# RG-LRU gate products on four 64-by-64 tiles of the TensorE array, with the conv result also kept with its halves exchanged

## The chip, the cores and the metric

The kernel runs on one core of a Trainium2 chip. The metric is the device time of one execution in microseconds (us), the median of several. TensorE is written PE, VectorE DVE, ScalarE ACT, GpSimd POOL, SyncE SP, as in the profile; PEld is PE's weight loads, and a q behind a name is that engine's instruction queue (its DMA issues and waits).

## The reference, cut to what matters

One layer over 2048 latent tokens and 256 context tokens: a modulated norm, one projection into four groups, an S5 branch, an RG-LRU branch, gating, an output projection, a norm. The part that changes is the gates of the RG-LRU branch, 16 heads of 64 channels:

```python
xh = xc.reshape(bsz, length, LRU_HEADS, LRU_HEAD_DIM)
r = sigmoid(einsum("blhi,hij->blhj", xh, w_a) + b_a)
gi = sigmoid(einsum("blhi,hij->blhj", xh, w_x) + b_x)
log_a = -LRU_C * r * softplus(-lam)
a = exp(log_a)
bx = sqrt(-expm1(2.0 * log_a)) * (gi * xc)
h[t] = a[t] * h[t-1] + bx[t]        # both directions, from the context's final state
```

`xc` is the result of a depthwise convolution of width 4. Each direction has its own `w_a` and `w_x`, one 64x64 matrix per head.

## The kernel before, in words

The program writes its instructions from Python generators. A framework then orders them for each engine by priorities and its own estimate of readiness; the order is fixed when the program is built. Each engine works its list in that order.

The first 560 us are the first half of the input projection with its preparation. Then comes the stretch that the change touches. `projections(1, ...)` projects the second half of the tokens: 128 steps, each of 12 matmuls of 128x128x512, named `pp` (lines 249 to 251). Each new weight block is split on DVE into `whi` and `wlo` (lines 241 and 242). Beside it `lru` works through 8 blocks of 128 channels (two heads each). One block is:

- `load` fetches the projected block into `ut` (one buffer), on SP's queue, after small memsets on POOL;
- `conv` forms `xc` (one buffer): one ACT instruction (line 367), then three on DVE (line 370), each over all 2307 columns;
- `gates` multiplies `xc` by the gate matrices, for both directions `d` and for five column pieces (259 and four of 512). A 128x128 matrix `gw` holds two heads on its diagonal and zeros elsewhere. The products go to two PSUM pools of two buffers each (`pg`), and ACT takes the sigmoids to `rr` and `gi` (line 381);
- ACT makes a Tanh into `tt` (line 424), an Exp in `rr` (line 431) and a Sqrt in `tt` (line 439), with a table load wherever the function set changes;
- `finish`, which runs during the gates of the next block, makes the two scans on DVE (lines 387 to 394), their sum (line 397) and the product with the SiLU gate (line 401).

`rr`, `gi` and `tt` have three buffers each, so the second direction of a block waits until `finish` of the block before has released one.

At the end of the generators stands `build`. It takes 8 projection steps alone, then 100 steps with `lru` beside them at 1.5 of its yields a step, then 8 steps with `s5_inputs` of the first S5 half (matmuls `pw`), then the last 12 steps with the second half's `s5_inputs` and the first of two S5 scans. A scan has 144 dependent steps of three DVE instructions (lines 729 to 731); the two scans overlap in part. `s5_outputs` (matmuls `py`) of a half needs that half's whole scan. The RG-LRU part of the output projection (matmuls `po`, 12 a step) fills PE between them. Two more projections (`pgl`, `po`) end the program.

## Time and profile before

| | us |
|---|---|
| median of 3 runs | 1852.38 (1851.83 to 1858.7) |
| the profiled execution's own time | 1850.69 |
| its span, first to last instruction | 1848.9 |
| PE busy | 1731.9 (94%) |
| DVE busy | 1208.6 (65%) |
| ACT busy | 864.0 (47%) |
| gate matmuls (line 380), 320 records | 135.8 |

A 32-bit matmul stands in the trace as two records, each with its weight load, so the 160 gate products are 320 records. Busy times count the union of records, and PE's records overlap, so a busy PE is not PE at its peak; idle time of an engine that others do not wait for costs nothing. The mean granted TensorE clock is 0.975 of full speed.

### The profile page before, as it was taken

What the parts mean: (1) busy time and instruction counts of PE and PEld (TensorE: products, weight loads), DVE (VectorE), ACT (ScalarE), POOL (GpSimd) and SP (SyncE); (2) the same over time, 40 slices, a digit from 0 to 9 for tenths busy, and PEclk for the clock granted to TensorE, in tenths of its full rate; (3) what the DMA queues carried; (4) which work ended last, traced back from release to release, by engine and by line L of the source; (5) the groups of instructions that cost most, each with busy time, mean ns of one, the idle gap of its engine ahead of it and who ended that gap; (6) DMA issues with size and microseconds to landing.
All of it is one profiled execution on the core that took longest, in us unless ns stands there. A gap on an engine that the chain in (4) does not pass through costs nothing. (4 is left out here: it accounts for less than half of the span.)

```text
span 1848.9 us, 25310 instructions
## 1 busy us (share of the span) xinstructions
PE 1731.9 (94%) x9465; PEld 1410.6 (76%) x9465; DVE 1208.6 (65%) x1998; ACT 864.0 (47%) x1350; POOL 117.8 (6%) x236
## 2 busy tenths in 40 slices
PE   7889999999998999999989997959899999999998
PEld 2677888878886666666668886748788899998886
DVE  5789997861244799999982199999900166346663
ACT  3622222223653867776754986225455443222221
POOL 1011121110000000000000000000000000001111
PEclk9899999999999999999999998979899999999999
DMA  9566676655454234344467876328688767456553
GB/s 268 128 141 214 195 204 168 194 179 165 132 164 154 75 125 137 120 143 120 114 179 233 272 241 205 120 70 261 203 272 262 227 184 211 140 158 216 185 194 88
DMA packets 356974, 326.34 MB, mean 177 GB/s; under 512 B 123774, under 2 KB 300530, under 8 KB 351731
## 3 DMA queue, kind: packets, MB, share of 16 engines
q1 hardware_dynamic: 309680, 221.41, 42.3%
q0 software_dynamic: 15040, 60.31, 9.0%
q10 hardware_dynamic: 32130, 43.01, 6.7%
q8 instruction: 75, 1.23, 0.3%
q14 instruction: 49, 0.39, 0.1%
HBM read 211.47 MB, written 113.18 MB: 176 GB/s over the span
## 5 line engine op out<-in xcount | busy, mean ns | idle before, releaser
L249 PE MATMUL pp<-x,whi 128*128 128x512 f32 x1024 | 417.2, 408 | 2.5 <-ACT ust L299 1.7
L251 PE MATMUL pp<-x,wlo 128*128 128x512 f32 x1024 | 407.4, 398 | 5.3 <-DVE wlo L242 5.3
L250 PE MATMUL pp<-x,whi 128*128 128x512 f32 x1024 | 406.5, 397 | 0.0
L242 DVE TENSOR_TENSOR wlo<-wraw,whi 128x1024 fp32r<-128x1024 f32 x90 | 109.9, 1221 | 192.8 <-ACT whi L241 146.0
L249 PEld LDWEIGHTS pp<-x,whi 128*128 128x128 f32 x1024 | 193.4, 189 | 54.1 <-issue 10.8
L251 PEld LDWEIGHTS pp<-x,wlo 128*128 128x128 f32 x1024 | 193.2, 189 | 50.7 <-DVE wlo L242 5.7
L250 PEld LDWEIGHTS pp<-x,whi 128*128 128x128 f32 x1024 | 193.2, 189 | 46.0 <-issue 6.3
L380 PE MATMUL pg<-xc,gw 128*128 128x512 f32 (+1 forms) x320 | 135.8, 572 | 18.6 <-issue 12.4
L241 ACT CAST whi<-wraw 128x1024 fp32r<-128x1024 f32 x66 | 69.2, 1049 | 164.7 <-PE pp L250 127.1
L380 PEld LDWEIGHTS pg<-xc,gw 128*128 128x128 f32 x320 | 61.2, 197 | 79.1 <-issue 57.5
L729 DVE TENSOR_TENSOR p<-z,A 128x128 f32<-128x128 f32 x288 | 106.3, 381 | 6.1
L764 PE MATMUL py<-h,et 128*128 128x128 f32 x512 | 81.0, 282 | 28.8 <-ACT h L757 14.8
L249 PE MATMUL po<-x,whi 128*128 128x512 f32 x256 | 105.5, 412 | 2.3 <-ACT x L794 2.3
L251 PE MATMUL po<-x,wlo 128*128 128x512 f32 x256 | 102.1, 399 | 4.8 <-DVE wlo L242 4.8
L250 PE MATMUL po<-x,whi 128*128 128x512 f32 x256 | 101.8, 397 | 1.8 <-DVE x L795 1.8
L249 PE MATMUL po<-ws,yh 128*128 128x512 f32 x256 | 99.6, 389 | 0.0
L250 PE MATMUL po<-ws,yh 128*128 128x512 f32 x256 | 99.6, 389 | 0.0
L251 PE MATMUL po<-ws,yl 128*128 128x512 f32 x256 | 99.6, 389 | 0.0
L764 PEld LDWEIGHTS py<-h,et 128*128 128x128 f32 x512 | 69.4, 197 | 31.3 <-ACT h L757 16.6
L701 PE MATMUL pw<-u,wt 128*128 128x144 f32 x512 | 73.2, 302 | 16.2 <-DMA wt<-WD 10.7
L701 PEld LDWEIGHTS pw<-u,wt 128*128 128x128 f32 x512 | 70.4, 202 | 20.8 <-issue 12.1
L730 DVE TENSOR_TENSOR z<-z,p 128x64 f32<-128x64 f32 x288 | 75.1, 273 | 10.9 <-ACT z L705 4.8
(255 smaller groups left out, 3479.2 us busy)
## 6 DMA issues: line engine op xcount, KB each, us to landing
wraw<-in_w_in_dram SPq DMA_DIRECT2D x74, 512.0 KB
u<-ZU SPq DMA_DIRECT2D x64, 288.0 KB
ED<-E POOLq DMA_DIRECT2D x16, 1024.0 KB, 4.3
WD<-Wt POOLq DMA_DIRECT2D x32, 512.0 KB, 3.9
wt<-WD SPq DMA_DIRECT2D x32, 512.0 KB
et<-ED SPq DMA_DIRECT2D x32, 512.0 KB
mt<-KD SPq DMA_DIRECT2D x64, 192.0 KB
wmod<-in_w_mod_dram SPq DMA_DIRECT2D x8, 1024.0 KB
```

What stands on the lines that cost most here:

```text
L241: copy(out=hi, in_=raw)
L242: self.nc.vector.tensor_sub(out=lo, in0=raw, in1=hi)
L249: nc.tensor.matmul(ps, lhsT=whi(k), rhs=xhi(k), start=(k == 0), stop=False)
L250: nc.tensor.matmul(ps, lhsT=whi(k), rhs=xlo(k), start=False, stop=False)
L251: nc.tensor.matmul(ps, lhsT=wlo(k), rhs=xhi(k), start=False, stop=(k == KT - 1))
L380: nc.tensor.matmul(ps[:, :n], lhsT=gw[:, d, w, :], rhs=xc[:, o:o + n], start=True, stop=True)
L701: nc.tensor.matmul(pw[:, c, :], lhsT=w[:, gi, kt, c, :], rhs=u[:, kt, :], start=(kt == 0), stop=(kt == 1))
L729: v.tensor_mul(out=p, in0=cur.unsqueeze(1).to_broadcast([P, 2, 2, 32]), in1=self.A16[:, :, :, gs])
L730: v.tensor_add(out=nxt, in0=nxt, in1=p[:, 0])
L764: nc.tensor.matmul(o, lhsT=ms(e[:, i, gi]), rhs=h[:, i, :], start=False, stop=(i == 1))
```

## The change

The gate matrix loses its zero blocks: `gw` holds, on partitions 0 to 63, the two heads of `w_a` and, on 64 to 127, those of `w_x`. `conv` also keeps `xs`, a copy of `xc` with its two halves of 64 partitions exchanged, made by two DMAs on POOL's queue; it takes the buffer of `ut`. A piece of both gates is now four matmuls of 64x64, each on its own quarter of the array: rows by the gate, columns by the head. Rows 0 to 63 (the first gate) read head 0 from `xc` and head 1 from `xs`; rows 64 to 127 (the second) read head 0 from `xs` and head 1 from `xc`. The interleaving with the projection is renumbered from 100 steps at 1.5 to 108 at 1.4. The two memsets of `gw` go.

```diff
-            gw = le.tile([P, 2, 2, P], F32, tag="gw", bufs=2, name="gw")
-            nc.gpsimd.memset(gw[0:64, :, :, 64:128], 0.0)
-            nc.gpsimd.memset(gw[64:128, :, :, 0:64], 0.0)
+            gw = le.tile([P, 2, 2, 64], F32, tag="gw", bufs=2, name="gw")
...
-                    nc.sync.dma_start(out=gw[es, :, w, es], in_=src)
+                    nc.sync.dma_start(out=gw[w * 64:w * 64 + 64, :, e, :], in_=src)
...
-            return xc
+            xs = le.tile([P, N + 3], F32, tag="ut", bufs=1, name="xs")
+            for e in range(2):
+                nc.gpsimd.dma_start(out=xs[e * 64:e * 64 + 64, :N], in_=xc[64 - e * 64:128 - e * 64, :])
+            return xc, xs
...
             for o, n in [(0, X0)] + (tl_x if d == 0 else tl_x[::-1]):
+                pss = [pool.tile([P, 512], F32, tag=tag, name="pg") for pool, tag in ((self.psG, "g"), (self.psT, "t"))]
+                for w in range(2):
+                    ws = slice(w * 64, w * 64 + 64)
+                    for e in range(2):
+                        nc.tensor.matmul(pss[w][e * 64:e * 64 + 64, :n], lhsT=gw[ws, d, e, :],
+                                         rhs=xcs[(w + e) % 2][ws, o:o + n], start=True, stop=True,
+                                         tile_position=(64 * w, 64 * e))
                 for w, dst in ((0, rr), (1, gi)):
-                    pool, tag = ((self.psG, "g"), (self.psT, "t"))[w]
-                    ps = pool.tile([P, 512], F32, tag=tag, name="pg")
-                    nc.tensor.matmul(ps[:, :n], lhsT=gw[:, d, w, :], rhs=xc[:, o:o + n], start=True, stop=True)
-                    nc.scalar.activation(out=dst[:, o:o + n], in_=ps[:, :n], func=AF.Sigmoid, bias=bias[w])
+                    nc.scalar.activation(out=dst[:, o:o + n], in_=pss[w][:, :n], func=AF.Sigmoid, bias=bias[w])
...
-                    merge(islice(proj, 100), [lru, 1.5])
+                    merge(islice(proj, 108), [lru, 1.4])
```

**PE's order.** In the fifth block the gate products of before stand in one run of 13, from both gates in turn, and the projection's `pp` follow; these are the end of that run and what comes behind it.

```order
L380 MATMUL pg_5802<-xc_5708,gw_5652 128x512
L380 MATMUL pg_5805<-xc_5708,gw_5652 128x512
L380 MATMUL pg_5808<-xc_5708,gw_5652 128x512
L380 MATMUL pg_5811<-xc_5708,gw_5652 128x512
L380 MATMUL pg_5831<-xc_5708,gw_5652 128x259
L380 MATMUL pg_5834<-xc_5708,gw_5652 128x259
L380 MATMUL pg_5854<-xc_5708,gw_5652 128x512
L251 MATMUL pp_5872<-x2_4241,wlo_5796 128x512
L249 MATMUL pp_5872<-x2_4241,whi_5797 128x512
```

In the changed kernel the same block begins with two products from `xc` alone (the first gate's pieces of 259 and 512), then 18 `pp`, and then these rows; behind them the other 32 tiles stand with 7 `pp` among them.

```order
L383 MATMUL pg_6138<-xs_6103,gw_6045 64x259
L383 MATMUL pg_6170<-xs_6103,gw_6045 64x512
L251 MATMUL pp_6303<-x3_4426,wlo_6164 128x512
L249 MATMUL pp_6303<-x3_4426,whi_6165 128x512
L250 MATMUL pp_6303<-x3_4426,whi_6165 128x512
L251 MATMUL pp_6303<-x3_4426,wlo_6164 128x512
L249 MATMUL pp_6303<-x3_4426,whi_6165 128x512
L383 MATMUL pg_6178<-xc_6098,gw_6045 64x512
L383 MATMUL pg_6178<-xs_6103,gw_6045 64x512
L383 MATMUL pg_6201<-xc_6098,gw_6045 64x512
L383 MATMUL pg_6201<-xs_6103,gw_6045 64x512
```

The order now runs ahead with the first gate; the products of a piece's second gate no longer stand behind those of its first.

**ACT's order.** The sigmoids of that block alternated between `rr` and `gi`.

```order
L381 ACTIVATE gi_5745<-pg_5749,vcol128_367 128x259
L381 ACTIVATE rr_5744<-pg_5754,vcol128_367 128x512
L381 ACTIVATE gi_5745<-pg_5757,vcol128_367 128x512
L301 DMA U_57<-ust_5851 128x512
L381 ACTIVATE rr_5744<-pg_5773,vcol128_367 128x512
L381 ACTIVATE gi_5745<-pg_5776,vcol128_367 128x512
```

They now come in groups, four of `rr` before the first of `gi` in the first direction.

```order
L387 ACTIVATE rr_6136<-pg_6178,vcol128_367 128x512
L387 ACTIVATE rr_6136<-pg_6201,vcol128_367 128x512
L387 ACTIVATE gi_6137<-pg_6139,vcol128_367 128x259
L387 ACTIVATE gi_6137<-pg_6171,vcol128_367 128x512
L387 ACTIVATE gi_6137<-pg_6179,vcol128_367 128x512
L387 ACTIVATE gi_6137<-pg_6202,vcol128_367 128x512
L387 ACTIVATE rr_6136<-pg_6225,vcol128_367 128x512
L430 ACTIVATE tt_6358<-rr_6136,c8h_693 128x2307
```

The number of sigmoids is the same; what moved is that the first direction's `gi` come last.

**POOL's order.** Before, between the output of one block (`YL`) and the next stood the memsets of `ut` and `gw`.

```order
L403 DMA YL<-rr 128x2048
L358 MEMSET ut 128x1
L359 MEMSET ut 128x3
L360 MEMSET ut 128x2
L347 MEMSET gw 64x4x64
L348 MEMSET gw 64x4x64
```

Now the two exchange DMAs stand there, and the memsets of `ut` behind them wait for the last gate product that reads `xs`.

```order
L409 DMA YL<-rr 128x2048
L371 DMA xs<-xc 64x2307 x2
L355 MEMSET ut 128x1
L356 MEMSET ut 128x3
L357 MEMSET ut 128x2
```

So the load of `ut` for the next block, which could start when the convolution was done, now starts after the block's gates.

## Rows read from the trace of the kernel before

**Rows 1.** Windows: two stretches, busy us of each engine, clock, DMA.

```profile
core 0: us, PE busy (x) PEld busy (x) DVE busy (x) ACT busy (x) POOL busy (x), PEclk, DMA share, GB/s
580.00:1001.00 421.00, 397.17 (x1473) 278.94 (x1472) 349.77 (x183) 285.85 (x299) 10.36 (x41) 0.98 0.44 134
...
1061.00:1340.00 279.00, 232.35 (x1288) 201.48 (x1287) 260.40 (x894) 140.26 (x261) 4.78 (x9) 0.91 0.60 185
```

**Rows 2.** Windows: six inner blocks, the first block, the last with its tail.

```profile
629.60:910.70 281.10, 264.71 (x960) 181.54 (x960) 256.64 (x133) 204.22 (x211) 8.22 (x34) 0.98 0.41 129
590.60:629.60 39.00, 38.97 (x142) 26.57 (x143) 19.54 (x12) 33.37 (x34) 1.07 (x5) 1.00 0.26 81
910.70:1001.50 90.80, 85.22 (x336) 64.27 (x336) 65.10 (x36) 44.68 (x51) 1.06 (x2) 0.96 0.63 177
```

**Rows 3.** Waits of PE, 629.6 to 910.7: us in total, times, longest.

```profile
PE pg L380 <- issue: 10.6, 4, 4.3
PE pg L380 <- ACT rr L381: 5.7, 4, 2.4
```

**Rows 4.** Waits of ACT, the same stretch.

```profile
ACT rr L381 <- DVE tt L394: 17.5, 4, 5.8
ACT tt L424 <- DVE tt L397: 11.1, 4, 4.2
```

**Rows 5.** Timeline of DVE, block four: start us, us, instruction, idle before.

```profile
721.07 2.62 DVE L370 SCALAR_TENSOR_TENSOR xc<-ut,vcol,xc 128x2307 f32<-128x2307 f32 x1
...
745.88 2.30 DVE L397 TENSOR_TENSOR tt<-tt 128x2048 f32<-128x2048 f32 x1
...
766.17 2.62 DVE L370 SCALAR_TENSOR_TENSOR xc<-ut,vcol,xc 128x2307 f32<-128x2307 f32 x1
```

**Rows 6.** Timeline of ACT, the same block.

```profile
738.50 0.48 ACT L381 ACTIVATE rr<-pg,vcol 128x259 f32<-128x259 f32 x1 [4.04 <-DVE tt L394]
...
748.27 2.23 ACT L424 ACTIVATE tt<-rr,c8h 128x2307 f32<-128x2307 f32 x1 [1.94 <-DVE tt L397]
...
757.96 2.31 ACT L367 ACTIVATE xc<-ut,vcol 128x2307 f32<-128x2307 f32 x1
```

**Rows 7.** Windows of tile pg: PE, PEld and ACT busy over all eight blocks.

```profile
590.60:930.90 340.30, 135.19 (x319) 61.24 (x320) 97.19 (x159) 0.98 0.38 119
```

**Rows 8.** Tile pg: duration of one, ns, min/median/max.

```profile
L381 ACT ACTIVATE rr<-pg,vcol x80: 463/687/708, 591.3 to 930.7; 128x512 f32<-128x512 f32 x64, 128x259 f32<-128x259 f32 x16
```

**Rows 9.** Windows of tile pp: an undisturbed stretch.

```profile
700.00:723.00 23.00, 23.00 (x102) 18.71 (x100) 0.69 (x1) 1.74 (x4) 1.00 0.49 166
```

**Rows 10.** Timeline of PE: 64-by-32 tiles of the S5 tables between full matmuls.

```profile
341.81 0.66 PE L631 MATMUL psk<-E,BR 64*32 64x256 f32 x16
342.26 0.64 PE L631 MATMUL psk<-E,BI 64*32 64x256 f32 x16
342.83 0.50 PE L249 MATMUL pp<-x,whi 128*128 128x512 f32 x1
343.17 0.39 PE L250 MATMUL pp<-x,whi 128*128 128x512 f32 x1
```

**Rows 11.** DMA issues on POOL's queue: count, KB each, median us to landing.

```profile
ED<-E POOLq DMA_DIRECT2D x16, 1024.0 KB, 4.3
WD<-Wt POOLq DMA_DIRECT2D x32, 512.0 KB, 3.9
```

**Rows 12.** Timeline of SP's queue: the issue of a 1,024 KB load.

```profile
745.87 0.32 SPq L400 DMA_DIRECT2D gi<-GL  x1
```

**Rows 13.** Timeline of DVE: the instruction that waited for that load.

```profile
751.95 2.29 DVE L401 TENSOR_TENSOR rr<-tt,gi 128x2048 f32<-128x2048 f32 x1 [0.71 <-DMA gi<-GL]
```

**Rows 14.** Windows of line 729 (one per scan step): DVE busy and steps.

```profile
1061.00:1164.70 103.70, 33.00 (x87) 0.92 0.71 224
1164.70:1243.00 78.30, 38.03 (x108) 0.85 0.23 75
1243.00:1340.00 97.00, 34.92 (x92) 0.94 0.77 233
```

**Rows 15.** Waits of PE, 1142 to 1470.

```profile
PE py L764 <- ACT h L757: 14.8, 2, 14.0
```

**Rows 16.** Windows of tile po: an undisturbed stretch.

```profile
1464.00:1482.00 18.00, 18.00 (x80) 14.89 (x80) 0.00 (x0) 1.76 (x3) 1.00 0.81 248
```

More of the change, by code (lines that the diff above doesn't have):

```diff
@@ L351, in weights @@
                     src = self.io[name][0, :, 2 * b + e].rearrange("d i j -> i d j")
-                    es = slice(e * 64, e * 64 + 64)
-                    nc.sync.dma_start(out=gw[es, :, w, es], in_=src)
+                    nc.sync.dma_start(out=gw[w * 64:w * 64 + 64, :, e, :], in_=src)
             return gw
@@ L371, in conv, with gates @@
                                        in1=xc, op0=ALU.mult, op1=ALU.add)
-            return xc
-        def gates(b, d, gw, xc, rr, gi):
+            xs = le.tile([P, N + 3], F32, tag="ut", bufs=1, name="xs")
+            for e in range(2):
+                nc.gpsimd.dma_start(out=xs[e * 64:e * 64 + 64, :N], in_=xc[64 - e * 64:128 - e * 64, :])
+            return xc, xs
+        def gates(b, d, gw, xcs, rr, gi):
             bias = [self.col[n][:, d * 8 + b:d * 8 + b + 1] for n in ("lru_b_a", "lru_b_x")]
             for o, n in [(0, X0)] + (tl_x if d == 0 else tl_x[::-1]):
+                pss = [pool.tile([P, 512], F32, tag=tag, name="pg") for pool, tag in ((self.psG, "g"), (self.psT, "t"))]
[5 more added lines that the diff above has]
+                                         tile_position=(64 * w, 64 * e))
                 for w, dst in ((0, rr), (1, gi)):
-                    pool, tag = ((self.psG, "g"), (self.psT, "t"))[w]
-                    ps = pool.tile([P, 512], F32, tag=tag, name="pg")
-                    nc.tensor.matmul(ps[:, :n], lhsT=gw[:, d, w, :], rhs=xc[:, o:o + n], start=True, stop=True)
-                    nc.scalar.activation(out=dst[:, o:o + n], in_=ps[:, :n], func=AF.Sigmoid, bias=bias[w])
+                    nc.scalar.activation(out=dst[:, o:o + n], in_=pss[w][:, :n], func=AF.Sigmoid, bias=bias[w])
                 yield
@@ L406, in lru @@
         gw = weights(0)
-        xc = conv(0, load(0))
+        xcs = conv(0, load(0))
         yield
@@ L414, in lru @@
                 gi.append(big("gi", 3))
-                for i, _ in enumerate(gates(b, d, gw, xc, rr[d], gi[d])):
+                for i, _ in enumerate(gates(b, d, gw, xcs, rr[d], gi[d])):
                     if i % 2 == 0:
@@ L426, in lru @@
             for d in range(2):
-                v.tensor_mul(out=gi[d], in0=gi[d], in1=xc)
+                v.tensor_mul(out=gi[d], in0=gi[d], in1=xcs[0])
             yield
@@ L434, in lru @@
             if b < 7:
-                gw, xc = gw2, conv(b + 1, ut)
+                gw, xcs = gw2, conv(b + 1, ut)
             yield
```

## Prediction

> **What bounds the kernel now.** I read the windows first, to see which engine is dense in which stretch. From 580 to 1001 us the RG-LRU branch runs beside the projection, with PE busy for 397 of 421 us; from 1061 to 1340 the S5 scans run, with DVE busy for 260 of 279 [rows 1]. The change lies in the first of these, so its six inner blocks were cut out: 281.1 us, 46.85 us a block, with PE at 44.1, DVE at 42.8 and ACT at 34.0 us a block [rows 2]. Two engines are over 90% busy, and neither is full.
>
> The waits say what couples them. PE loses 16.3 us in the six blocks, 10.6 where the first gate product stands behind the convolution and 5.7 where a PSUM buffer waits for a sigmoid [rows 3]. ACT in its turn waits 17.5 us for a scan that frees `rr` and 11.1 us for the sum that frees `tt` [rows 4]. The timeline of one block shows the loop behind that. The convolution of the fourth block ends on DVE at 723.69; the sum at line 397, last of the preceding block's scan work, ends at 748.18; ACT's Tanh starts at 748.27, its share of the next convolution at 757.96, and that convolution ends on DVE at 768.79 [rows 5, 6]. This is 45.1 us once round, with no matmul in it. The gates run inside it, with room: the second direction's first sigmoid waited 4.04 us for DVE [rows 6]. So PE sets the pace only in part, and a shorter gate product is not simply time gained.
>
> **The change part by part.** *Gate products.* A `pp` takes 23.0 / 102 = 0.2255 us [rows 9], an inner block has 120 of them (720 of the 960 records), 27.1 us, which leaves 17.0 us of PE's 44.1 for the gates; the gate records alone give 135.19 / 8 = 16.9 [rows 7]. Per column and pass (9,228 columns, two passes) that is 0.92 ns, so 0.48 us for a product of 259 columns and 0.94 us for one of 512. If four tiles run side by side, a piece of both gates costs one product instead of two, 8.5 us a block. That tiles do so is seen in the S5 tables: eight tiles of 64 rows by 32 columns, two passes of 256 columns each, take 0.45 us from one set to the next [rows 10]; one pass is 0.235 us by the rate above, so tiles that took turns would need 3.8 us, and those of the same rows alone 1.9 us.
>
> A rule speaks against this pairing. In the Trainium skill, page "TensorE: Matmul & The Clock Gate", section "Part 3: Packing small matmuls — row/col tiling", a weight load overlaps running matmuls only if it goes to other rows of the array. Here tiles of the same rows follow each other in pairs, and by that rule the pairs would go one after the other; the sum by it is the fourth rival's, some 1900 us. The 0.45 us of the trace, with four tiles on the same rows, does not agree, and the sum goes by the trace.
>
> *Changes between full array and tiles.* Two sets of tiles took 1.02 us for four passes (0.94 us), and the `pp` behind came 0.34 us after its predecessor instead of 0.2255 [rows 10]: about 0.2 us for going there and back. The changed order has 38 runs of gate tiles, under five a block: 1.0 us. Lower bound nothing; upper bound the 0.34 us on both sides of each run, 3.2 us a block. I take 1.0, as measured.
>
> *More projection.* At 1.4 yields a step a block's 15 yields take 10.7 steps instead of 10: 8.6 more `pp`, 1.9 us. PE's bare work becomes 44.1 - 16.9 + 8.5 + 1.0 + 1.9 = 38.6 us a block.
>
> *But PE walks through the gates at ACT's pace.* A block has 20 sigmoids, 16 of 0.687 us and four of 0.463 [rows 8], 12.8 us, with two PSUM buffers a gate. By the order, two tiles and then, 18 `pp` later, their partners run alone (2 x 1.42 us), two more pairs of the first gate run alone (1.9 us), and the rest goes with the remaining 16 sigmoids (10.3 us) and one Tanh of 2.2 us [rows 6] among them, of which PE need not wait out the last 1.4 us: 11.1. Together 15.8 us, hardly under the 16.9 of before. PE's way through a block is then 27.1 + 1.9 + 15.8 = 44.8 us. Without the Tanh or the runs ahead of the first gate it would be 41 (lower bound); with every wait of before kept (2.7 us a block) 47.5.
>
> *The exchange.* Two DMAs of 577 KB go out when the convolution ends. Nothing before copies from SBUF to SBUF; the nearest rows of that queue land after 3.9 us (512 KB) and 4.3 us (1,024 KB) [rows 11]. I take 4.0 us for the first and, as they follow each other, 5 us for the second. PE needs the first after 1.42 + 18 x 0.2255 + 0.2 = 5.7 us and the second some 3 us later, so it costs nothing. Hiding it are the 18 `pp`; without them 4 us a block. Upper bound: both share the engines and come one after the other with the load of a large tile beside them, 9.4 us, 3.7 us late. Queued behind the stalled tile are all `pp` of PE, and behind those the splits on DVE.
>
> *The load of `ut`* now waits for the last gate product. A load of 1,024 KB was there 6.1 us after its issue at most [rows 12, 13]; ACT came to the convolution 19.5 us after the second direction's first sigmoid [rows 6], of which the ten sigmoids take 6.4 [rows 8], so it costs nothing, or up to 2 us if the loads ahead of it on SP's queue (`gi` from `GL`) are still moving. The memsets of `gw` on POOL go; nothing there was late.
>
> *DVE's order.* Its instructions are the same; the split for 8.6 more `pp` adds 0.4 us to 42.8, so 43.2 us a block is a floor.
>
> *The sum to the S5 part.* Three lower limits stand close: 43.2 (DVE), 44.8 (PE through the gates), 45.1 (the loop). I take 45.0 us a block: 6 x (45.0 - 46.85) = -11.1 us. The first block, PE's own at 39.0 [rows 2], has 17 more `pp` and some 2 us less in gates: +1.8. Behind the last gates stand 306 `pp` instead of 276: +6.8. The S5 part starts 2.5 us earlier.
>
> *What the eight moved steps do later.* They leave the scan stretch, where PE waited 14 us for the first scan anyway [rows 15], so nothing is gained by that itself. But the second scan starts after 74 steps of the first instead of 90, by the order on DVE. A lone step costs about 97.0 / 92 = 1.05 us, an overlapped one 78.3 / 108 = 0.725 [rows 14]. The first scan then takes 74 x 1.05 + 12.4 (the other DVE work in that stretch, 103.7 - 87 x 1.05) + 133 x 0.725 = 186.5 us instead of 182.0: +4.5. And 60 `po` move from behind the last `py` to the wait ahead of the first (336 instead of 276 there): -60 x 0.225 [rows 16] = -13.5 us.
>
> Total -2.5 + 4.5 - 13.5 = -11.5 us: 1850.69 becomes 1839.2, and as the median of the runs lies 1.7 us above the profiled execution, **1841 us**.
>
> **The rivals.** A measurement here tells some 0.5% (9.3 us) from no change, so "same" is 1843.1 to 1861.6.
>
> *The loop keeps its pace, 46.85 us.* For it: ACT and DVE have the same instructions in nearly the same order. Against it: 5.7 us of PE's waits and those of ACT for gate products shrink. Then -0.4 us: 1852.
>
> *PE was the brake and DVE's floor is reached,* 43.5 us a block. For it: both are over 90% busy. Against it: the loop of 45.1 us. Inner blocks -20.1: 1832.
>
> *The exchange ends on the path (slower).* At the 9.4 us above, PE stands 3.7 us in each of eight blocks, since it takes its list in order: -11.5 + 29.6 = +18, less the 2.5 us by which the loop then has PE's other waits: 1868. It decides from 1.4 us late (landing 7.1 us after the convolution), and is clearly slower from 2.6. Against it: 3.9 and 4.3 us [rows 11].
>
> *Tiles of the same rows take turns.* The gates then need 17.0 us with both gates side by side and 5.6 more for what runs ahead alone, 23.6 with the changes: 52.6 us a block, inner blocks +34, first and last +23: about 1900.
>
> **How the numbers follow.** My forecast 0.36, the unchanged loop 0.25, DVE's floor 0.17, the late exchange 0.17, tiles taking turns 0.05. A spread of 8 us about 1841 straddles the bound, two thirds of it faster. Faster: 0.17 + 0.25 = 0.42; same: 0.25 + 0.11 + 0.03 of the late exchange = 0.39; slower 0.19. The range goes from under the DVE floor's 1832 to the late exchange's 1868: 1826 to 1868; the forecast's own is 1833 to 1849.
>
> **What would show it.** Gate tiles starting in pairs and quartets within 0.1 us, and gate time on PE of 8 to 11 us a block; sigmoids back to back in the second direction; `pg` waiting for `xs` under 1 us a block; inner blocks at 45 us with DVE over 94%; a first `pw` some 400 to 411 us after the first gate product; 14 us fewer behind the last `py`. Wrong it would be by `xs` landing after 7 us, by a block period that does not move, by the granted clock (0.98 here [rows 2]) falling where PE waits within the gates, or by a scan stretch that takes up the 13.5 us.

## The result: slower by 1.24%, and the profile after

The changed kernel takes 1877.1 us (median of 4 runs, 1871.3 to 1882.3) against 1852.3 for the kernel before: ratio 1.0124, 95% interval 1.0104 to 1.0145. The forecast was 1841 with a range up to 1868. The profiled execution took 1877.3 us, 26.6 more than that of before.

The windows after, cut as in [rows 2] (first block, six inner blocks, last block with its tail), show where: all three parts are longer, by 5.9, 10.9 and 10.4 us. An inner block takes 48.67 us instead of 46.85.

```profile
core 0: us, PE busy (x) PEld busy (x) DVE busy (x) ACT busy (x) POOL busy (x), PEclk, DMA share, GB/s
594.80:639.70 44.90, 43.05 (x200) 26.57 (x201) 20.27 (x13) 32.76 (x34) 1.20 (x5) 1.00 0.36 97
639.70:931.70 292.00, 276.18 (x1236) 169.48 (x1236) 258.43 (x134) 202.42 (x214) 10.49 (x36) 0.96 0.54 154
931.70:1032.90 101.20, 96.42 (x417) 70.16 (x418) 67.98 (x38) 48.75 (x56) 2.12 (x4) 0.95 0.65 186
```

These 27.2 us are a little more than the whole loss. The first gate product came 4.2 us later than before, and from the first `pw` to the end 4.8 us were won. I count the 4.2 us as spread: as many `pp` stand ahead of the first gate product in both, and tiles_old_merge (below), which has the changed kernel's gates and exchange, has it at 591.0 us.

The waits of PE and ACT in the six inner blocks (us in total, times, longest) answer to [rows 3] and [rows 4]. PE's are as short as before, 12.4 us instead of 16.3. ACT's have changed sides: before, it waited 28.6 us for DVE [rows 4] and 24.4 us for gate products (the two rows of before shown first); now it waits 7.1 us for DVE and 56.6 us for gate products. PE has become the later one.

```profile
ACT rr L381 <- PE pg L380: 19.6, 39, 2.1
...
ACT gi L381 <- PE pg L380: 4.8, 22, 1.0
```

```profile
PE pg L383 <- ACT gi L387: 4.1, 7, 1.5
PE pg L383 <- issue: 4.1, 3, 2.8
PE pg L383 <- ACT rr L387: 3.0, 2, 1.5
PE pg L383 <- DMA xs<-xc: 1.2, 1, 1.2
...
ACT rr L387 <- PE pg L383: 49.8, 23, 9.9
...
ACT tt L430 <- DVE tt L403: 7.1, 3, 3.4
ACT gi L387 <- PE pg L383: 6.8, 17, 1.3
```

Over the whole stretch the windows of the tiles `pg` and `pp` say how much of each there is: 640 passes of gate tiles, and 1212 projection products instead of 1116.

```profile
594.80:1032.90 438.10, 126.45 (x640) 36.66 (x640) 93.67 (x160) 0.96 0.55 155
594.80:1032.90 438.10, 293.64 (x1212) 229.35 (x1212) 8.81 (x13) 28.89 (x50) 0.96 0.55 155
```

Busy time is no good measure of a matmul's price here, since a record's modelled end overlaps the next record. What follows therefore counts *taken* time: from the start of one PE record to the start of the next, less the idle time between. By that the gates took 118.7 us before and 123.8 after, the `pp` 270.2 and 291.9, and PE stood idle for 22.0 and 22.5: the sums are 410.9 and 438.2. So the tiles saved PE nothing, and the 96 moved products cost it 21.7 us.

Why the tiles saved nothing is in PE's timeline of the second block (start us, us, instruction, count).

```profile
639.67 1.48 PE L383 MATMUL pg<-xc,gw 64*64 64x259 f32 x4 [0.63 <-issue]
...
645.61 1.51 PE L383 MATMUL pg<-xs,gw 64*64 64x259 f32 x4
648.18 0.64 PE L383 MATMUL pg<-xc,gw 64*64 64x512 f32 x1
648.18 0.64 PE L383 MATMUL pg<-xs,gw 64*64 64x512 f32 x1
648.66 0.59 PE L383 MATMUL pg<-xc,gw 64*64 64x512 f32 x1
648.66 0.59 PE L383 MATMUL pg<-xs,gw 64*64 64x512 f32 x1
649.09 0.59 PE L383 MATMUL pg<-xc,gw 64*64 64x512 f32 x1
```

At 639.67 two tiles that read `xc` run one behind the other (the same quarter of the array, for two pieces), at 645.61 their neighbours that read `xs`. At 648.18 two tiles start together, on the same rows, but only two. A pass of 512 columns takes 0.43 to 0.51 us whether one, two or (below) four tiles are in it. Counting passes that start within 0.12 us of the first one as one set, the 640 passes make 297 sets: 80 of one tile, 142 of two, 24 of three, 51 of four. Before there were 320 passes, one by one.

The exchange's row (issue to landing, us) shows a median of 7.2. It mixes two kinds: the first transfer of a block landed 4.8 to 6.5 us after its issue (5.5 to 7.1 us after the convolution's end), the second 7.9 to 10.5 us (9.1 to 11.6). I had put 4.0 and 5.

```profile
xs<-xc POOLq DMA_DIRECT2D x16, 576.8 KB, 7.2
```

The later part in three pieces (first `pw` to last `py`, to the first `pgl`, to the end), of the kernel before and then of the changed one:

```profile
1001.50:1463.80 462.30, 407.64 (x2450) 360.15 (x2448) 277.74 (x911) 264.95 (x502) 7.44 (x14) 0.94 0.69 214
1463.80:1483.00 19.20, 19.20 (x88) 15.89 (x87) 4.72 (x4) 6.26 (x8) 0.55 (x1) 1.00 0.76 233
1483.00:1848.90 365.90, 356.83 (x2305) 326.52 (x2303) 195.07 (x324) 100.82 (x199) 29.55 (x61) 0.99 0.57 172
```

```profile
1032.90:1493.90 461.00, 396.98 (x2412) 353.19 (x2411) 265.36 (x907) 260.06 (x497) 7.97 (x15) 0.96 0.68 209
1493.90:1506.70 12.80, 5.75 (x27) 4.44 (x25) 0.02 (x1) 2.27 (x4) 0.53 (x1) 0.83 0.70 201
1506.70:1875.50 368.80, 359.70 (x2304) 329.15 (x2304) 199.38 (x328) 102.25 (x201) 29.02 (x60) 0.99 0.58 174
```

From the first `pw` to the last `py` 38 fewer matmul records change 1.3 us. The 60 `po` that left the second piece saved 6.4 us there, not 13.5, since 7.1 us of it is now a wait of `pgl` for ACT's `yh`, and the last piece is 2.9 us longer.

### The profile page after: what moved, and what is told of

The parts are those of the page before. It is cut to its first block, busy times and chain, and to the rows that moved or that the text cites. A ratio compares the mean times of both kernels' runs of the same rounds, so it can differ in the third digit from the quotient of the medians.

```text
span 1875.5 us, 25968 instructions
## 1 busy us (share of the span) xinstructions
PE 1740.4 (93%) x9785; PEld 1391.0 (74%) x9785; DVE 1201.0 (64%) x1998; ACT 857.9 (46%) x1351; POOL 119.8 (6%) x236
## 4 chain that ended last, share of the span: by engine, by line
PE 61%; DVE 18%; DMA 7%; ACT 7%; issue 6%; SPq 1%; POOL 0%; ACTq 0%; DVEq 0%; POOLq 0%
PE pp L249 9%; PE pp L251 9%; PE pp L250 9%; DVE p L735 5%; PE po L249 4%; PE po L251 4%; PE po L250 4%; PE pg L383 4%; PE pgl L249 3%; PE pgl L250 3%; PE pgl L251 3%; DVE z L737 3%; DVE z L736 3%; PE py L770 2%; PE py L768 2%
## 5 line engine op out<-in xcount | busy, mean ns | idle before, releaser
L250 PE MATMUL pp<-x,whi 128*128 128x512 f32 x1024 | 409.0, 399 | 0.0
L383 PE MATMUL pg<-xc,gw 64*64 64x512 f32 (+1 forms) x320 | 114.2, 596 | 12.7 <-issue 5.7
L383 PE MATMUL pg<-xs,gw 64*64 64x512 f32 (+1 forms) x320 | 110.5, 588 | 7.9 <-ACT gi L387 6.5
L250 PE MATMUL po<-x,whi 128*128 128x512 f32 x256 | 101.4, 396 | 0.0
L707 PEld LDWEIGHTS pw<-u,wt 128*128 128x128 f32 x512 | 68.7, 199 | 30.5 <-issue 14.8
L770 PEld LDWEIGHTS py<-h,et 128*128 128x128 f32 x512 | 69.8, 198 | 25.6 <-ACT h L763 14.4
L768 PE MATMUL py<-u,mt 128*128 128x128 f32 x512 | 80.1, 280 | 0.0
```

The lines of the kernel that those rows point to most:

```text
L250: nc.tensor.matmul(ps, lhsT=whi(k), rhs=xlo(k), start=False, stop=False)
L383: nc.tensor.matmul(pss[w][e * 64:e * 64 + 64, :n], lhsT=gw[ws, d, e, :], rhs=xcs[(w + e) % 2][ws, o:o + n], start=True, stop=True, tile_po ...
L707: nc.tensor.matmul(pw[:, c, :], lhsT=w[:, gi, kt, c, :], rhs=u[:, kt, :], start=(kt == 0), stop=(kt == 1))
L768: nc.tensor.matmul(o, lhsT=ms(m[:, i * 8:i * 8 + T]), rhs=u[:, i, 16:], start=(i == 0), stop=False)
L770: nc.tensor.matmul(o, lhsT=ms(e[:, i, gi]), rhs=h[:, i, :], start=False, stop=(i == 1))
```

## The experiments

Eighteen more kernels ran. The table gives the ratio to the kernel before on the same chip with its 95% interval; then, from the profile, the stretch from the first gate product to the first `pw` as first block / inner block (mean of six) / last block with tail; then PE's taken time in that stretch for gates and `pp`, and its idle time. Six of the kernels compute something other than the reference: exchange_only and the five with no_exchange in their names. In the stretch tiles_together_100 has 24 `pp` fewer than the 1116 of before, hybrid_100 and hybrid_conv_early_100 have 9 fewer.

| kernel | ratio (interval) | stretch: parts, us | gates / pp / idle, us |
|---|---|---|---|
| before | 1 | 410.9: 39.0 / 46.85 / 90.8 | 118.7 / 270.2 / 22.0 |
| changed | 1.0124 (1.0104-1.0145) | 438.1: 44.9 / 48.67 / 101.2 | 123.8 / 291.9 / 22.5 |
| before_new_merge | 1.0102 (1.0085-1.0119) | 432.2: 39.1 / 48.13 / 104.3 | 114.8 / 295.8 / 21.6 |
| before_less_moved | 1.0074 (1.0049-1.0098) | 388.8: 39.0 / 45.41 / 77.3 | 123.3 / 242.1 / 23.4 |
| tiles_old_merge | 1.0019 (1.0005-1.0034) | 414.2: 46.5 / 47.36 / 83.5 | 124.0 / 266.9 / 23.4 |
| tiles_no_exchange | 1.0069 (1.0054-1.0084) | 428.0: 35.8 / 48.23 / 102.9 | 94.7 / 293.5 / 39.9 |
| tiles_no_exchange_100 | 1.0002 (0.9988-1.0017) | 408.9: 35.9 / 46.91 / 91.6 | 102.6 / 266.2 / 40.0 |
| exchange_only | 1.0060 (1.0039-1.0080) | 418.6: 42.8 / 47.06 / 93.4 | 122.5 / 271.0 / 25.1 |
| tiles_together_100 | 1.0113 (1.0076-1.0150) | 417.4: 48.4 / 51.71 / 58.7 | 123.3 / 266.7 / 27.4 |
| spread_108 | 1.0477 (1.0450-1.0504) | 468.8: 60.2 / 58.87 / 55.4 | 92.1 / 303.4 / 73.3 |
| spread_100 | 1.0456 (1.0432-1.0480) | 460.5: 59.9 / 58.24 / 51.2 | 93.9 / 281.8 / 84.8 |
| spread_108_no_exchange | 1.0130 (1.0104-1.0157) | 409.0: 48.9 / 50.85 / 54.9 | 82.0 / 301.3 / 25.6 |
| spread_full_100 | 1.0200 (1.0166-1.0234) | 422.9: 54.7 / 52.58 / 52.7 | 101.4 / 292.2 / 29.3 |
| before_conv_early | 0.9991 (0.9978-1.0005) | 408.9: 34.6 / 46.59 / 94.7 | 113.6 / 274.5 / 20.8 |
| hybrid_100 | 1.0016 (1.0000-1.0032) | 409.8: 39.5 / 46.37 / 92.0 | 119.7 / 263.6 / 26.4 |
| hybrid_conv_early_100 | 1.0033 (1.0016-1.0049) | 413.0: 33.0 / 48.13 / 91.2 | 112.1 / 268.2 / 32.8 |
| tiles_conv_early_100 | 1.0048 (1.0032-1.0064) | 414.6: 40.7 / 46.87 / 92.7 | 117.1 / 275.0 / 22.5 |
| spread3_no_exchange_100 | 0.9997 (0.9983-1.0012) | 411.2: 39.7 / 47.94 / 83.8 | 88.3 / 280.2 / 42.7 |
| spread3_hybrid_100 | 1.0081 (1.0051-1.0110) | 427.4: 42.4 / 48.54 / 93.8 | 100.9 / 288.2 / 38.3 |
| no_exchange_conv_early_100 | 0.9964 (0.9948-0.9981) | 404.8: 31.5 / 46.40 / 94.9 | 94.7 / 272.8 / 37.3 |

The theory (T1 in the expectations) was that PE's list in order is the pace, that tiles take as much of it as full products, and that the moved products are therefore paid in full. The rivals: T2, the pace is VectorE and ScalarE, so that moved products are free; T3, the exchange alone makes the loss.

### The change taken apart

Old numbers in the changed kernel:

```diff
-                    merge(islice(proj, 108), [lru, 1.4])
+                    merge(islice(proj, 100), [lru, 1.5])
```

> The changed kernel with the old numbers in the merge (100 projection steps at 1.5, instead of 108 at 1.4), all else as changed. T1, TensorE's list is the pace of the RG-LRU stretch and the gate products on four tiles take as much of it as the full ones, so that the eight projection steps moved ahead add 96 products of 0.227 us (22 us) to it: from the first gate product to the first pw falls from 438 us back to 411-418 us, and the whole to 1853-1863 us. T2, VectorE and ScalarE are the pace, so the moved steps were free and the loss lies in the new gates or the exchange: no change against the changed kernel, 1872-1880 us. T3, the exchange of the halves is the cause: also 1872-1880 us.

New numbers, the same edit backwards, in the kernel before:

> The kernel before with nothing but the new numbers in the merge (108 projection steps at 1.4); full gate products with the zero blocks, no exchange. T1 (TensorE's list is the pace, moved steps are paid in full there): six inner blocks 295-303 us instead of 281, stretch up to the first pw about 433 us instead of 411, some of it given back in the scan, in all 1860-1875 us. T2 (the loop of VectorE and ScalarE is the pace): six inner blocks 281-284 us, 1842-1853 us. T3 (the exchange): 1842-1853 us too.

And the old numbers moved by as much the other way in the kernel before (`92`, `1.63`):

> The kernel before with 92 projection steps at 1.63 in the merge instead of 100 at 1.5: the same edit as the eight moved steps, the other way. If TensorE's list is the pace of the RG-LRU stretch down here too, 96 products of 0.227 us less make the stretch up to the first pw 389-396 us instead of 411, and what follows takes at least as long as before (460 us from the first pw to the last py, some 6 us more ahead of pgl): 1837-1852 us. If VectorE's 43.2 us a block or the loop of conv and gates is right behind, the stretch falls by 8 us at most, and with the work that now lies behind it the whole is 1850-1868 us.

T1 held in the first two and T2 fell: the numbers alone make the kernel before 1.02% slower (18.9 us), and without them the change costs 0.19% (3.5 us). Together that is the change's 1.24% within the intervals. Only the inner blocks of before_new_merge, at 288.8 us, fell short of T1's 295 to 303. Its windows show the place: one third of the 21.3 us in the inner blocks, two thirds behind the last gates, where 36 more `pp` stand.

```profile
591.10:630.10 39.00, 39.00 (x143) 26.77 (x144) 19.55 (x12) 33.35 (x34) 1.03 (x5) 1.00 0.26 81
630.10:918.90 288.80, 274.69 (x1013) 191.21 (x1012) 258.25 (x135) 207.32 (x215) 7.64 (x34) 0.99 0.41 129
918.90:1023.30 104.40, 96.91 (x379) 72.84 (x379) 68.03 (x38) 48.55 (x55) 1.07 (x2) 0.97 0.61 173
```

The moved steps bring DVE and ACT work along (4.6 and 7.0 us more busy time in the stretch), and no run here moves one without the other. That PE's list is what they lengthen is read from PE's own account: 21.7 us more taken, 0.4 less idle.

The third run missed in the whole (1837 to 1852 us expected, 1865 measured), and of the three numbers tried the old ones are best. With 96 products fewer the stretch is 22.1 us shorter, as T1 has it, but from the first `pw` to the last `py` it takes 482.8 us instead of 462.3, and 30.1 instead of 19.2 from there to the first `pgl`: 0.74% slower in all.

The exchange taken out of the changed kernel (and, below, out of it with the old numbers):

```diff
-            xs = le.tile([P, N + 3], F32, tag="ut", bufs=1, name="xs")
-            for e in range(2):
-                nc.gpsimd.dma_start(out=xs[e * 64:e * 64 + 64, :N], in_=xc[64 - e * 64:128 - e * 64, :])
-            return xc, xs
+            return xc, xc
```

> The changed kernel without the exchanged copy: all four tiles of a gate product read xc in place, so that two of the four multiply the other head's half (a changed computation), and no exchange transfer, no wait for one and no second use of ut's buffer are left; merge at 108 and 1.4. T1: the eight moved steps still cost their 22 us less what contiguous quartets save on TensorE (a quartet in 0.45 us where the two lone halves took more, up to 8 us a block), so 1855-1872 us. T3, the exchange alone is the cause: 1835-1848 us, with six inner blocks at 265-275 us. T2: 1872-1880 us, since the sigmoids and VectorE's work are the same.

> The changed kernel without the exchange (all four tiles read xc in place, a changed computation) and with the old numbers in the merge: the most that tiles can give in this order. Against the kernel with the same tiles and 1212 products it has 96 products less ahead of the first pw. If TensorE's list is the pace with tiles too, the stretch falls by the full 22 us, to about 406 us, and the whole to 1845-1850 us; if the loop of conv and gates has become the pace once the exchange is gone, it falls by under 10 us, 1856-1864 us.

The exchange put into the kernel before, where the second gate's product reads it:

```diff
-                    nc.tensor.matmul(ps[:, :n], lhsT=gw[:, d, w, :], rhs=xc[:, o:o + n], start=True, stop=True)
+                    nc.tensor.matmul(ps[:, :n], lhsT=gw[:, d, w, :], rhs=(xc, xs)[w][:, o:o + n], start=True, stop=True)
```

> The kernel before with its full gate products and old merge numbers (100 at 1.5), and the exchanged copy made in ut's buffer and read by the second gate's product (a changed computation: the input gate works on the exchanged halves). T1: the exchange shows as a few us of waits of TensorE a block at most, 1850-1858 us. T3, the exchange costs the loss by itself: 1868-1880 us.

The exchange costs 0.55% (10 us) in the changed kernel and 0.60% (11 us) beside full products; with the old numbers it is 0.17% (3 us), where the two intervals overlap. T3 has a share, and in exchange_only a larger one than T1 gave it. Without the exchange 3 of the sets are of one tile instead of 80, the gates take 94.7 us of PE instead of 123.8, and ACT waits for them for 25.3 us in the inner blocks instead of 49.8, and for DVE again (rows of tiles_no_exchange):

```profile
ACT rr L384 <- PE pg L380: 25.3, 22, 3.2
ACT rr L384 <- DVE tt L397: 25.2, 5, 7.6
```

With the new numbers these tiles without an exchange are 0.33% (6 us) under full products (1.0069 against 1.0102, the intervals apart). The surprise is tiles_no_exchange_100, where they win nothing (1.0002, between its two forecasts). PE's gates take 102.6 us instead of 118.7, and the stretch is 408.9 instead of 410.9: PE's idle time has grown by 18 us. The windows of its inner blocks show PE 13 us less busy than in [rows 2], DVE as busy as there, the granted clock at 0.94 instead of 0.98 and the block at 46.9 us; the waits of PE below them name the sigmoids' buffers.

```profile
629.10:910.50 281.40, 251.30 (x1200) 160.24 (x1199) 256.55 (x133) 199.61 (x211) 5.13 (x24) 0.94 0.41 129
```

```profile
PE pg L380 <- ACT rr L384: 18.4, 6, 4.4
PE pg L380 <- issue: 5.6, 2, 3.9
```

Its 640 passes still fall into 241 sets, 152 of two tiles and 75 of four, though nothing waits for an exchange. The tiles of one gate share a PSUM buffer that one sigmoid frees, and the other gate's buffer is freed one sigmoid later; in a run without projection products between them the fours come apart into pairs. That reading of the timeline is argued here; the next runs bear on it.

### A list written out

The four tiles ordered behind each other, those on `xs` first, but otherwise in the scheduler's list:

```diff
+                mm = None
+                for w, e in ((0, 1), (1, 0), (0, 0), (1, 1)):
+                    with self.tc.issue_after(mm.ins) if mm else nullcontext():
+                        mm = nc.tensor.matmul(...)
```

> The changed kernel with the old numbers in the merge, and the tiles that read the exchanged copy first in each four, the others behind them, so that hardly any tile runs by itself while the exchange is on its way. By the trace of the changed kernel a four in a burst takes TensorE 1.33 us and a run of two lone tiles 1.55 us, so that a block's gates fall from 15.5 to about 13.6 us, 15 us over the eight; but all gates now wait for the exchange (4.8 to 10.5 us after the conv). If TensorE's list is what counts, 1838-1850 us; if the loop of conv, exchange and gates takes back what the list gives, 1853-1870 us.

It missed: 1.13% slower than before. All gates wait for the exchange, the first ones starting 5.4 to 6.3 us behind the conv, with 112 to 123 `pp` put ahead of them in five of the blocks; of its 268 sets 107 were still of one tile and 103 of three.

In the next four kernels PE's list is fixed: a gate product's tiles (or the two full products), then six `pp`, and so on, with 84 or 96 `pp` between a block's last gates and the next block's first. A gate product goes behind the last `pp` traced (`self.last`), each of its tiles behind the one before (not shown), and `next(steps, None)` traces six `pp`. The lines are those of spread_108, in part.

```diff
+                with self.tc.issue_after(self.last.ins):
+                    for w, e in ((0, 1), (1, 0), (0, 0), (1, 1)):
+                        self.lastg = nc.tensor.matmul(...)
...
+                    for kind in lru:
+                        if kind == "gate":
+                            with self.tc.issue_after(self.lastg.ins):
+                                next(steps, None)
+                        else:
+                            owed += 3
+                            drain(islice(steps, int(owed)))
```

> The changed kernel with the same 1212 projection products ahead of the first pw, but TensorE's list written out: the four tiles of a gate product stand together and six projection products stand between one four and the next, instead of fours in bursts with lone tiles ahead of them. If it is the bursts that make the tiles cost as much as the full products (sigmoids at 1.6 us for each four pace TensorE, tiles run alone while the exchange is on its way, the clock falls), TensorE needs about 1212 x 0.227 + 80 x 0.45 + 80 x 0.2 = 327 us there, VectorE's 43.2 us a block ends last, the stretch up to the first pw is 390-415 us and the whole 1828-1855 us. If tiles cost TensorE as much wherever they stand, or the loop of xc, exchange, gates and conv is the pace, the stretch stays at 430-440 us and the whole at 1868-1880 us.

> The same written-out list with the old amount of projection work (1116 products ahead of the first pw). If TensorE is still the pace there, about 20 us less than with 1212; if VectorE's floor or the loop of xc, exchange and gates has become the pace, the stretch up to the first pw is the same within 4 us in both, and the whole within 6 us. By bursts as the cause: 1830-1852 us; by tiles that cost as much wherever they stand: 1850-1860 us.

> The written-out list with 1212 projection products, and all four tiles reading xc in place (a changed computation: two of the four multiply the other head's half), no exchange. If the exchange is hidden by the projection products between the conv and the gates, the same as with the exchange within 4 us; if the loop through the exchange is the pace, some 5 us less a block, 25-40 us in all.

> The kernel before (full gate products with zero blocks, no exchange, 1116 projection products) in the same written-out list: two full products, then six projection products. It tells what the list alone does, without tiles. If the tiles are what frees TensorE once they are spread, this one is 15-25 us slower than the spread tiles with 1116; if the list alone does it, the two are the same within 5 us, both under the kernel before.

All four missed: they are 4.77%, 4.56%, 1.30% and 2.00% slower than before. The last, with full products and no exchange, shows that such a list costs time by itself.

But here the price of a four (the four tiles of one gate product) can be read undisturbed. In spread_108_no_exchange it starts at 649.36, the next `pp` at 650.38, and that one holds PE for 0.34 us instead of 0.23; in spread_full_100 the two full products take from 657.33 to 658.64, and the `pp` behind them 0.63.

```profile
649.36 1.09 PE L382 MATMUL pg<-xc,gw 64*64 64x512 f32 x8
650.38 0.50 PE L249 MATMUL pp<-x,whi 128*128 128x512 f32 x1
```

```profile
657.33 1.88 PE L383 MATMUL pg<-xc,gw 128*128 128x512 f32 x4
658.64 0.79 PE L249 MATMUL pp<-x,whi 128*128 128x512 f32 x1
659.27 0.39 PE L250 MATMUL pp<-x,whi 128*128 128x512 f32 x1
```

So a four costs 1.02 + 0.11 = 1.13 us and two full products 1.31 + 0.40 = 1.71: a third less, not half (the medians over 61 such places in each kernel are 1.13 and 1.72). And 151 of 169 sets are now of four. With 1212 products and no exchange the gates take 82.0 us of PE instead of 94.7, and the stretch is 409.0 us, 19 less than the same tiles in the scheduler's list, though more than that is lost again behind it (below). With the exchange, each block's gates wait for it, and without projection work among the waiting there is nothing to do: the stretch of spread_108 is 59.8 us longer than that of its twin without the exchange, and the number of `pp` hardly matters (8.3 us for 96). PE stands idle after each convolution until the first transfer has landed, and again until the second has. Its waits in the six inner blocks, all at these places whichever releaser the row names, are these:

```profile
PE pg L385 <- issue: 41.2, 8, 9.1
PE pg L385 <- DMA xs<-xc: 14.9, 4, 5.0
```

All four also lose 27 us from the first `pw` to the last `py` (489 to 490 us instead of 462). With 96 or 108 `pp` behind the last gates instead of 276 the last block's work on DVE and ACT is not covered, and the S5 part's first buffers wait for its output; the row is from spread_108_no_exchange:

```profile
ACT z L709 <- DMA YL<-rr: 22.4, 1, 22.4
```

That was a flaw of the lists, not of the tiles, so two more keep 260 `pp` for the end, with three `pp` between gate products; one without the exchange, one for the whole computation with full products in the first direction and tiles in the second (`if d == 0` full, as in hybrid_100 below).

> A written-out list again, with three projection products between one gate product's four tiles and the next, 90 between a block's last and the next block's first, and 261 behind the last block's gates as in the kernel before; 1116 projection products, all tiles on xc in place (a changed computation), no exchange. It tells what tiles give at most. If a four that has products behind it costs TensorE 1.13 us against 1.72 for two full products (as read from the written-out lists so far), and the bursts' wait for the sigmoids is filled by the three products, TensorE's occupied time is 80 x 1.13 + 1116 x 0.227 = 344 us; with VectorE's 43.2 us a block the stretch up to the first pw is 370-395 us and the whole 1815-1838 us. If the sigmoids or the loop of conv and gates hold the blocks at what they have now, 405-412 us and 1848-1856 us.

> The same list for the whole computation: the first direction's gates by full products on xc while the exchange is on its way, the second direction's on four tiles, three projection products between one and the next, 1116 in all. If the list of before loses to bursts what tiles can win, TensorE's occupied time is 40 x 1.72 + 40 x 1.13 + 253 = 367 us, the stretch 385-405 us and the whole 1828-1848 us, under both kernels; if the blocks are held by sigmoids and the loop, 1850-1860 us.

The first fell on its second branch: it takes as long as the kernel before, although its gates take 30 us less of PE, since the idle time took 21 of them and the `pp` 10. The second is 0.81% slower and missed both of its ranges.

### Which pace holds the blocks

If not PE's work, then a loop might: from a block's last gate product to the end of the next conv it took 155 to 180 us (the seven together) in all kernels up to here, whatever `pp` lay between, and except where they waited for the exchange the gates began mostly 0.1 us behind the conv. So the conv was moved ahead of the two Exps on ACT, and the Exps ordered behind its activation (`self.cact`):

```diff
             yield
+            if b < 7:
+                gw, xc = gw2, conv(b + 1, ut)
+                th = self.cact
+            yield
             with self.tc.issue_after(th.ins):
                 for d in range(2):
                     ex = nc.scalar.activation(out=rr[d], in_=rr[d], func=AF.Exp,
...
-            yield
-            if b < 7:
-                gw, xc = gw2, conv(b + 1, ut)
```

> The kernel before with one thing moved: a block's conv stands ahead of the two Exps on ScalarE instead of behind them. Its xc is written over the old one, so it still waits for the last products with it. Loop theory (the pace is the loop first gate product, last gate product, conv, next gate product; its part from the last gate product to the end of the conv was 22 to 25 us in every run so far, whatever projection work lay in it): that part falls by the 4 to 6 us of the two Exps, to 18-20 us, the stretch up to the first pw by 10-25 us until TensorE's 389 us of occupied time or VectorE's 43.2 us a block ends last, and the whole to 1828-1845 us. List theory (TensorE's order of products is the pace everywhere and the conv follows it): the same 411 us and 1848-1856 us.

> All gates on tiles as in the changed kernel, old numbers in the merge, and the conv ahead of the Exps. By the loop theory the loop still holds the exchange (5.5 us), so its part from the last gate product to the next first one falls by 4 to 6 us but the gates' own part stays at 24 us: stretch 395-405 us instead of 414, whole 1838-1850 us, slower than with full products and the same early conv. List theory: 414 us and 1855-1860 us.

Full products in the first direction, tiles in the second, to take the exchange off the path, without and with the early conv:

```diff
                 for w in range(2):
+                    if d == 0:
+                        nc.tensor.matmul(pss[w][:, :n], lhsT=gw[0][:, w, :], rhs=xcs[0][:, o:o + n],
+                                         start=True, stop=True)
+                        continue
```

> The old numbers in the merge; the first direction's gates by full products on xc, the second direction's on four tiles, so that the exchange is on its way while the first five pairs of products run and no tile stands alone. Against the kernel with all gates on tiles and the old numbers it takes the exchange off the loop: if the exchange and the lone tiles are what made tiles no gain there, 1845-1853 us, the same or a little under the kernel before; if tiles lose for another reason (changes of tile shape, half clock), 1856-1862 us as with all gates on tiles.

> Both edits: the conv ahead of the Exps, and the second direction's gates on four tiles behind the first direction's full products, old numbers in the merge. By the loop theory the loop is short enough here for TensorE's own work to count, and five fours save some 1.5 to 3 us a block over full products: 3 to 20 us under the kernel with the early conv alone, 1820-1840 us. If tiles give TensorE nothing in this kernel, the same as with the early conv alone.

Last, no exchange and the early conv together:

> Both limits eased at once: all four tiles on xc in place (a changed computation, no exchange), which takes 16 to 20 us off TensorE's occupied time, and the conv ahead of the two Exps, which takes some 36 us off the sums of last gate product to end of conv; old numbers in the merge, 1116 projection products. Each edit by itself left the stretch up to the first pw at 409 us. If TensorE's list and the loop through conv and sigmoids stand close together and each held the stretch when the other was eased, the stretch falls to 385-400 us and the whole to 1826-1843 us. If a third thing holds it (VectorE's order, the pace of the sigmoids), 405-412 us and 1848-1856 us.

The loop theory fell. In before_conv_early the seven pieces from last gate product to conv did shrink from 167.1 to 131.1 us, and the gates' own part, over all eight blocks, grew from 172.3 to 209.3, with 344 `pp` among them instead of 164: the list puts its work elsewhere, and the stretch is 408.9 us. The windows of the inner blocks of before_conv_early and of no_exchange_conv_early_100:

```profile
626.20:905.70 279.50, 260.64 (x949) 179.35 (x948) 255.49 (x132) 198.30 (x210) 7.20 (x32) 0.98 0.40 127
```

```profile
625.40:903.80 278.40, 246.91 (x1191) 154.52 (x1190) 255.22 (x132) 195.95 (x210) 4.24 (x24) 0.94 0.41 128
```

With all gates on tiles the early conv leaves the stretch as it was too (414.6 us against 414.2) and the whole is 0.48% over before instead of 0.19%; hybrid_conv_early_100, forecast as the best of all, is slower than hybrid_100. With PE's gates and the loop eased at once a block still takes 46.4 us, the first alone is shorter (31.5 instead of 39.0), and the whole is 0.36% under before (0.19 to 0.52%), for a changed computation without the exchange. Among kernels that compute the reference none was measurably faster than before: before_conv_early is the same within 0.2%. Of those with tiles hybrid_100 (0.16% slower, at most 0.32) and tiles_old_merge (0.19%) come nearest to it.

## Why the prediction was wrong, by its own steps

*More projection, 1.9 us a block, costed as cover: the step that failed.* The sum took three lower limits (43.2, 44.8, 45.1) and let the moved `pp` and PE's waits vanish under 45.0. They did not: 96 products took 21.7 us of PE's list, and the kernel before with them alone loses 18.9 us. An inner block took 48.67 us instead of 45.0: on PE 15.7 of gates, 30.3 of `pp` and 2.7 idle, where before they were 14.9, 29.2 and 2.7. The moved products were paid, the waits stayed, and the gates did not get shorter. The prediction's own bound with every wait kept, 47.5, is the nearest; like the 44.8 it lacks the 1.0 us that the step on changes had just put down.

The blocks do not follow the largest of three separate limits: with 96 products more an inner block is 1.3 us longer, with 96 fewer 1.4 shorter, while DVE is at 42 to 43 us in all of them. Nor was 45.1 a limit. It is the fourth block's own length, from one convolution's end to the next; the six inner blocks of before are 44.4, 49.8, 45.1, 48.7, 44.4 and 48.7 us long by the same measure, and no row shows that the scan work ahead of 745.88 had to follow the convolution.

The first block went from 39.0 to 44.9 (forecast +1.8): its 17 more `pp` came as forecast, the 2 us less of gates did not, and PE was idle for 1.8. This part goes with the exchange and not with the new numbers, since before_new_merge has 39.1 us there and tiles_old_merge 46.5. The last part grew by 10.4 (forecast +6.8).

*Gate products, "one product instead of two".* For a four that stands alone a third of the time was saved (1.13 against 1.71 us), not half, and tiles on the same rows do start together, as [rows 10] had it. The rule of the Trainium skill (page "TensorE: Matmul & The Clock Gate", section "Part 3: Packing small matmuls — row/col tiling") that a weight load overlaps running matmuls only if it goes to other rows, by which the prediction had the pairs take turns, does not agree with the eight passes in 1.02 us. But in the changed kernel only 51 of 297 sets were fours. My base was too high as well: 16.9 us a block were busy time, 14.8 is what the gates took of PE. So 16.9 to 15.8 was in fact 14.8 to 15.5.

*The exchange, costed at nothing.* The first transfer landed 5.9 us after the convolution (median of the eight blocks), near the 5.7 at which PE was to need it; the second landed at 10.6, where PE was to need it at some 8.7 and the forecast had 5. It cost 10 us in this kernel. Not by PE waiting for `xs`, which is 1.2 us in the inner blocks, and so not in the way of its rival: it made tiles run alone, two in 1.5 us, and brought the gate products later to ACT, which waited for them twice as long as without the exchange. The 18 `pp` that were to hide it hid PE's wait and not ACT's.

*Changes between array and tiles* were near: a `pp` behind tiles came 0.34 us after its predecessor, as in [rows 10].

*The later part:* forecast -9.0, measured -4.8. The second scan's +4.5 us did not show; of the 13.5 us of moved `po` 6.4 came, less 2.9 behind it, and 1.3 came ahead of it.

*Right* was the caution that PE sets the pace only in part and a shorter gate product is not simply time gained. With the old numbers, tiles without an exchange freed 16 us of PE and won 2 in the stretch and nothing in the whole. What stays open is which wait holds an inner block at 46.4 to 47.9 us when PE has less to do. It is not PE's gate time and not the place of the conv, since taking either or both away left it within 0.5 us (46.4 to 46.9 instead of 46.85). DVE is busy for 42.5 to 43.1 us of the block in these runs, so its order and its short waits for ACT and PE are the nearest suspect: in tiles_no_exchange_100 ACT waits 35.8 us in the inner blocks for DVE's scans, 28.6 before. In spread3_no_exchange_100, though, ACT waits mostly for gate products (45.5 us), and no run here changed DVE's work by itself: before_less_moved has 0.9 us less of it a block and a block 1.4 us shorter, but 10 `pp` fewer too.

## What to carry to other kernels

Where two engines are over 90% busy and coupled block by block, as here, count work that is moved in as paid on the engine whose list it enters, and freed time there not yet as won: test the moved work by itself in the kernel before, it was one number here. Here small tiles paid on PE only where all tiles of a set were ready at the same time: count sets that really start together, and look whether their inputs and their PSUM buffers become free together. A copy that a shorter instruction needs lies on the path of all that waits for that instruction, even if the engine fills the time, as ACT's waits showed.

## What the runs showed of the hardware

Four tiles of 64 by 64 take 8 passes of 512 columns in 1.02 us, one tile alone 0.43 to 0.48 a pass, so the three other tiles come at next to no cost in a set. In the changed kernel the first of two transfers of 577 KB between partitions landed 4.8 to 6.5 us after its issue and the one behind it 7.9 to 10.5, against 3.9 us for 512 KB to memory in [rows 11].

TensorE's granted clock was lower in the kernels with tiles. In the inner blocks it is 0.98 of full speed before (part of the time at 1.2 GHz, the rest at 2.4), 0.96 in the changed kernel and 0.94 in tiles_no_exchange_100, where PE is busy 251 of 281 us, though the projection is the same. In the stretch the clock stood at the lower level for 17 us before, 31 in the changed kernel and 44 in tiles_no_exchange_100, 37 of these between a block's first and last gate product. The taken times above contain this; how much of what tiles free is given back in this way no run here took apart.
